# A third set of weight buffers, and weights fetched two ahead, in a two-layer attention and FFN trunk

## The chip, the cores and the metric

The kernel runs on one core of a Trainium2 chip. The metric is the device time of one execution in microseconds (us), as the median of several runs; a profile of one more execution shows where the time goes.

## What is computed

Two layers over a sequence of 512 tokens with a model width of 1024, all in float32. Each layer is a mixer and a gated FFN with a short causal convolution, each behind an RMS norm and added to x. The mixer of layer 0 is a sparse attention with three branches (compressed blocks, selected blocks, a window; NSA below), that of layer 1 a sliding-window attention (SWA). A last norm ends it. Cut from the reference:

```
for i in range(DEPTH):                       # DEPTH = 2
    h = rms_norm(x, norm_mix[i])
    x = x + (nsa_mixer(h, ...) if i % 2 == 0 else swa_mixer(h, ...))
    h = rms_norm(x, norm_ffn[i])
    x = x + conv_ffn(h, ffn_w_gu[i], ffn_conv_w[i], ffn_conv_b[i], ffn_w_down[i])
return rms_norm(x, norm_final)

def conv_ffn(h, w_gu, conv_w, conv_b, w_down):     # D_FF = 2816
    a, u = split(h @ w_gu, 2)
    a = causal_depthwise_conv(a, conv_w, conv_b)   # width 3
    return (silu(a) * u) @ w_down
```

## The kernel before, in words

x is held transposed, as eight chunks X[k] of 128 features x 512 tokens. A product in float32 is made of three matmuls in a reduced type (fp32r): every operand is split in a high part, its cast, and a low part, what the cast lost; then high x high, high x low part of x, and low part of the weight x high (`mm3_steps`, L200 to L207; its matmuls are L206). Chunks of x are split by L310 or L309 (`xh`) and L313 (`xl`).

**Weights.** `load_w` (L175 to L185) brings one weight of 128 x 1024: SP issues the transfer into a raw tile (`wraw`, L182, with a raised priority), ACT casts it to the high part (`wh`, L183), and DVE or POOL subtracts to the low part (`wl`, L184); `lo_eng`, or an argument, says which. The three tiles come from the pool `wp` (L148) with two buffers of each. In attention, weights come from a list `to_load` through `next_w` (L194 to L199), which hands out one and fetches the next. Elsewhere `load_w` is called where a weight is used: the first two weights of the kernel (L484), the two first products of each FFN (`first_products`), the plain gate/up products of each FFN (`plain`, L554, f = 0 to 3) and the down projection (`load_down`).

**The FFN's other products** (f = 4 on) follow a Strassen-like scheme with seven half-width products instead of eight: `operands` (L577 to L597) makes sums of chunks of the normed x on POOL (L585 to L588) and splits them (ACT L591, a copy into PSUM by ACT at L595, DVE L597 into `xs`); `weights(f)` (L599 to L621) makes sums of weights on POOL (L608), two of them into a tile with the tag `wraw`, casts them on ACT (L614) into a tile of the tag `wh` and others, and makes low parts on DVE (L620), of a copy in PSUM for some. So these sums use the pool `wp` too. TensorE multiplies at L631. After each gate/up product POOL multiplies the gate by the up part (L567 and its like at the end of `gate_up_7`).

**Order.** The code gives a program order and a few priorities; a scheduler then sets the order on every engine and queue, from dependencies, priorities and when the buffers of a tag come free. A buffer set that is larger changes where a load, its cast and its split stand among the other work. All transfers are issued by SP or ACT. Softmax heads in attention run with steps of weight products put in between (class `Fill`).

## Time and profile before

| | us |
|---|---|
| runs, median of 3 (lowest to highest) | 1260.33 (1257.42 to 1264.54) |
| profiled execution, its own time | 1261.37 |
| span of its profile | 1259.5 |
| busy in the span: TensorE (PE) | 1209.9 |
| busy: VectorE (DVE) | 890.4 |
| busy: ScalarE (ACT) | 788.3 |
| busy: GpSimd (POOL) | 565.1 |

The mean granted clock of TensorE is 0.993 of full speed. In the span the stages lie one after the other: the first loads and the norm to about 24 us, NSA to 348, a norm and the first FFN products to 375, the FFN to 730 (plain products to 410, seven-product scheme to 600, down projection after it), SWA from 735 to 866, and the second FFN to the end. SyncE (SP) only issues transfers. "Waits" below are idle times of an engine put down to what ended them; busy times count no waits.

### The profile page before, as it was taken

The page shows a single profiled execution, that of the slowest core. Times are in us where ns is not written, and L with a number is a line of the kernel's source. Part 1 is how long each engine was busy: PE and PEld are TensorE (multiplying, and loading weights), DVE is VectorE, ACT ScalarE, POOL GpSimd, SP SyncE. Part 2 cuts the span into 40 slices and gives each one's busy share as a digit, 9 for nine tenths or more (in the row PEclk, how much of TensorE's full clock was granted, in tenths as well). Part 3 has the DMA queues.
Part 4 walks back from the last instruction along what each step waited for, and adds up shares of the span by engine and source line. Part 5 has one row for each costly group of instructions (what it writes and reads, how often), then busy time and mean ns, then how long its engine had stood idle before and what let it go on. Part 6 is the DMA issues. An engine that isn't in the chain of part 4 may idle for free.

```text
span 1259.5 us, 20317 instructions
## 1 busy us (share of the span) xinstructions
PE 1209.9 (96%) x7174; PEld 1045.0 (83%) x7174; DVE 890.4 (71%) x1785; ACT 788.3 (63%) x1644; POOL 565.1 (45%) x441
## 2 busy tenths in 40 slices
PE   6999999999999899999999999999989999999997
PEld 4877996787878899999788887788779999988886
DVE  6476778878677988788633367997798887893223
ACT  4377676767559878878422225865688878873222
POOL 4295554534229566763000126322586667710002
PEclk9999999989999999999999999999999999999998
DMA  5856635041124323331233365422413333213333
GB/s 191 245 162 195 196 119 157 26 147 39 48 75 135 108 96 108 108 103 55 80 94 96 89 199 152 126 72 88 151 60 113 102 106 107 88 46 109 92 92 126
DMA packets 65910, 141.71 MB, mean 113 GB/s; under 512 B 8464, under 2 KB 16912, under 8 KB 65808
## 3 DMA queue, kind: packets, MB, share of 16 engines
q1 hardware_dynamic: 64432, 139.25, 35.9%
q8 instruction: 57, 0.93, 0.3%
q10 hardware_dynamic: 1376, 1.15, 0.3%
q14 instruction: 45, 0.37, 0.1%
HBM read 123.14 MB, written 17.24 MB: 111 GB/s over the span
## 4 chain that ended last, share of the span: by engine, by line
PE 67%; DVE 14%; issue 5%; DMA 5%; POOL 5%; ACT 4%; SPq 0%; POOLq 0%; ACTq 0%; DVEq 0%
PE mm L206 31%; PE mm L631 9%; PE s L631 7%; PE o L631 6%; DVE ls L620 2%; PE s L1177 1%; PE s L206 1%; PE t L1201 1%; PE o L1019 1%; DVE xl L313 1%; PE o L1322 1%; POOL wl L184 1%; DMA wraw<-in_w_gu 1%; DVE p L1196 1%; DVE p L1416 1%
## 5 line engine op out<-in xcount | busy, mean ns | idle before, releaser
L183 ACT CAST wh<-wraw 128x1024 fp32r<-128x1024 f32 (+3 forms) x136 | 126.2, 930 | 236.1 <-PE mm L206 143.3
L184 DVE TENSOR_TENSOR wl<-wraw,wh 128x1024 fp32r<-128x1024 f32 (+3 forms) x80 | 96.6, 1209 | 115.5 <-PE mm L206 68.6
L184 POOL TENSOR_TENSOR wl<-wraw,wh 128x1024 fp32r<-128x1024 f32 (+3 forms) x56 | 108.3, 1936 | 138.2 <-PE mm L206 77.0
L206 PE MATMUL mm<-xs,wh 128*128 128x512 f32 (+1 forms) x374 | 141.3, 383 | 2.3 <-DVE apad L635 2.3
L239 POOL TENSOR_TENSOR rt<-rt 128x512 f32<-128x512 f32 x22 | 31.5, 1430 | 197.7 <-ACT rt L233 197.5
L206 PE MATMUL mm<-xh,wh 128*128 128x512 f32 x264 | 107.3, 408 | 6.2 <-ACT wh L183 5.2
L206 PE MATMUL mm<-xl,wh 128*128 128x512 f32 x264 | 105.6, 401 | 3.8 <-DVE xl L313 3.8
L620 DVE TENSOR_TENSOR ls<-s,hs 128x512 fp32r<-128x512 f32 x72 | 90.4, 1266 | 3.1 <-ACT hs L614 1.9
L206 PE MATMUL mm<-xs,wl 128*128 128x512 f32 (+1 forms) x374 | 90.5, 382 | 0.0
L1187 ACT ACTIVATE p<-p,sm 128x128 f32<-128x128 f32 (+3 forms) x128 | 71.7, 562 | 22.7 <-DVE sm L1184 22.2
L631 PE MATMUL mm<-xs,hs 128*128 128x256 f32 x576 | 84.7, 284 | 0.5 <-DVE apad L635 0.5
L206 PEld LDWEIGHTS mm<-xs,wh 128*128 128x128 f32 x374 | 70.4, 188 | 17.4 <-DVE apad L635 2.7
L631 PE MATMUL o<-xs,ha 128*128 128x256 f32 x576 | 81.1, 283 | 1.9 <-ACT apad L641 1.9
L608 POOL TENSOR_TENSOR s<-u,u 128x512 f32<-128x512 f32 x36 | 48.5, 1347 | 72.8 <-DVE la L620 34.0
L206 PEld LDWEIGHTS mm<-xs,wl 128*128 128x128 f32 x374 | 67.6, 188 | 15.1
L631 PEld LDWEIGHTS mm<-xs,hs 128*128 128x128 f32 x576 | 76.0, 193 | 0.7 <-DVE apad L635 0.7
L631 PEld LDWEIGHTS o<-xs,ha 128*128 128x128 f32 x576 | 74.3, 192 | 2.5 <-ACT apad L641 2.3
L206 PE MATMUL mm<-xh,wl 128*128 128x512 f32 x264 | 70.1, 394 | 0.0
L1184 DVE CUSTOM_DVE_ANT_0 p<-s,cst 128x128 f32<-128x128 f32 (+3 forms) x128 | 58.5, 481 | 15.9 <-PE s L1177 8.6
L206 PEld LDWEIGHTS mm<-xh,wh 128*128 128x128 f32 x264 | 50.8, 193 | 17.4 <-ACT wh L183 5.2
L206 PEld LDWEIGHTS mm<-xl,wh 128*128 128x128 f32 x264 | 50.5, 192 | 15.6 <-DVE xl L313 6.3
L608 POOL TENSOR_TENSOR wraw<-a,u 128x512 f32<-128x512 f32 x36 | 57.3, 1591 | 7.4 <-ACT t L618 7.4
(369 smaller groups left out, 3538.4 us busy)
## 6 DMA issues: line engine op xcount, KB each, us to landing
u<-in_w_gu SPq DMA_DIRECT2D x72, 256.0 KB, 2.6
a<-in_w_gu SPq DMA_DIRECT2D x72, 256.0 KB, 2.7
wraw<-in_w_dn SPq DMA_DIRECT2D x34, 512.0 KB, 3.5
wraw<-in_w_nsa SPq DMA_DIRECT2D x19, 512.0 KB, 4.4
q<-d SPq DMA_DIRECT2D x32, 256.0 KB, 4.8
wraw<-in_w_gu SPq DMA_DIRECT2D x16, 512.0 KB, 3.7
wraw<-in_w_dn SPq DMA_DIRECT2D x17, 384.0 KB, 3.1
d<-rh SPq DMA_DIRECT2D x21, 256.0 KB, 2.4
```

Source lines behind the costliest of these rows:

```text
L183: nc.scalar.copy(wh[:, c], raw[:, c])
L184: (eng or lo_eng[0]).tensor_tensor(wl[:, c], raw[:, c], f32(wh[:, c]), op=ALU.subtract)
L206: nc.tensor.matmul(pt, ws[k][w], rs[k][r], start=first and i == 0, stop=last and i == len(ops) - 1, **kw)
L239: self.eng.tensor_tensor(self.acc, self.acc, sq, op=ALU.add)
L313: nc.vector.scalar_tensor_tensor(xl[k], xt, V(gain, k), f32(xh[k]), op0=ALU.mult, op1=ALU.subtract)
L608: nc.gpsimd.tensor_tensor(out, x, y, op=op)
L620: nc.vector.tensor_tensor(ws[o][1], w, f32(ws[o][0]), op=ALU.subtract)
L631: nc.tensor.matmul(pt, ws[o][w][:, i * P:(i + 1) * P], xs[:, o, i, x], start=start and n == 0, stop=n == len(ops) - 1, skip_group_check=True)
L1019: nc.tensor.matmul(acc[0][:, j * P:], v2[:, 2 * j + br], pp[:, 4 * j:4 * j + NT - j, :], start=br == 0 and j == 0 and pp is pts[0][0], sto ...
L1177: ins = nc.tensor.matmul(dst, ql, kk[:, :, :n] if shared else kk[:, br, :n], start=c.start == 0 and kk is kst[0], stop=kk is kst[-1], skip ...
L1184: nc.vector.tensor_tensor_reduce(pt[:, c], pss[:, c], mask[:, T - (c.stop - c.start):], -1.0, 3e38, ALU.add, ALU.min, st[:, u:u + 1])
L1187: nc.scalar.activation(pt[:, c], pt[:, c], AF.Exp, scale=-1.0, bias=st[:, u:u + 1], accum_out=st[:, 2 + u:3 + u])
```

## The change

The pool `wp` gets three buffers of each of its tags, 12 KB more per partition (3 tags x 128 x 1024 values of 4 bytes = 4 KB each), and the scratch that is kept for dynamic transfers is set to 4096. `next_w` fetches until two weights are loaded and not yet handed out, instead of one. As the same tags serve the FFN, its products have three sets as well. In the changed file, lines from L182 on stand one further down, and from L199 on two.

```diff
+W_BUFS = 3
...
-    wp = ctx.enter_context(tc.tile_pool(name="wp", bufs=2))
+    wp = ctx.enter_context(tc.tile_pool(name="wp", bufs=W_BUFS))
...
         w = loaded.popleft()
-        fetch_w()
+        while to_load and len(loaded) < W_BUFS - 1:
+            fetch_w()
         return w
...
-    nc = bacc.Bacc("TRN2", target_bir_lowering=False, num_devices=1)
+    nc = bacc.Bacc("TRN2", target_bir_lowering=False, num_devices=1, dynamic_dma_scratch_size=4096)
```

**Start of the kernel, SP's queue.** X are the eight chunks of x (L482, now L484), `wraw<-in_w_nsa` the raw weights (L182, now L183). Before:

```order
L482 DMA X<-in_x 128x512
L182 DMA wraw<-in_w_nsa 128x512 x2
L482 DMA X<-in_x 128x512
L182 DMA wraw<-in_w_nsa 128x1024
L482 DMA X<-in_x 128x512 x6
L182 DMA wraw<-in_w_nsa 128x1024
L487 DMA cst<-in_consts 128x384
```

Now:

```order
L484 DMA X<-in_x 128x512
L183 DMA wraw<-in_w_nsa 128x512 x2
L484 DMA X<-in_x 128x512
L183 DMA wraw<-in_w_nsa 128x1024
L484 DMA X<-in_x 128x512 x3
L183 DMA wraw<-in_w_nsa 128x1024
L484 DMA X<-in_x 128x512 x2
L183 DMA wraw<-in_w_nsa 128x1024
L484 DMA X<-in_x 128x512
L489 DMA cst<-in_consts 128x384
```

The third weight's load moved from behind all eight chunks to behind the fifth, and a fourth weight's load stands ahead of the eighth.

**Start of the kernel, DVE.** `xl_81` to `xl_88` are the low parts of chunks 0 to 7 (L313, now L315), `rt` the running sum of squares for the norm (L239, now L241), `wl` the low part of the third weight (L184, now L185). Before:

```order
L313 SCALAR_TENSOR_TENSOR xl_85<-X,vec,xh_77 128x512
L309 TENSOR_SCALAR xh_80<-X,vec 128x512
L313 SCALAR_TENSOR_TENSOR xl_88<-X,vec,xh_80 128x512
L239 TENSOR_TENSOR rt<-rt 128x512
L313 SCALAR_TENSOR_TENSOR xl_87<-X,vec,xh_79 128x512
L239 TENSOR_TENSOR rt<-rt 128x512 x3
L892 TENSOR_TENSOR ohl<-rt,ohl 128x8x48
L184 TENSOR_TENSOR wl<-wraw,wh 128x1024
```

Now:

```order
L315 SCALAR_TENSOR_TENSOR xl_86<-X,vec,xh_78 128x512
L185 TENSOR_TENSOR wl<-wraw,wh 128x1024
L241 TENSOR_TENSOR rt<-rt 128x512
L315 SCALAR_TENSOR_TENSOR xl_87<-X,vec,xh_79 128x512
L311 TENSOR_SCALAR xh_80<-X,vec 128x512
L241 TENSOR_TENSOR rt<-rt 128x512
L315 SCALAR_TENSOR_TENSOR xl_88<-X,vec,xh_80 128x512
L241 TENSOR_TENSOR rt<-rt 128x512
```

The third weight's split moved from behind the sums to ahead of the last two low parts of x, and one more sum stands ahead of the last. ACT's cast of that weight now stands ahead of the high part of the seventh chunk in the same way.

**Start of the first FFN, POOL.** `lu_4232<-ls_4230,ls_4231` (L588, now L590) is the last sum of the operands, `g` a gate product, L608 (now L610) sums of weights. Before:

```order
L608 TENSOR_TENSOR s_4332<-a_4328,wraw 128x512
L588 TENSOR_TENSOR lu_4232<-ls_4230,ls_4231 128x256
L608 TENSOR_TENSOR wraw<-s_4485,a_4481 128x512
L608 TENSOR_TENSOR wraw<-a_4481,u_4483 128x512
L567 TENSOR_TENSOR g_4226<-g_4226,y 128x512
L608 TENSOR_TENSOR s_4486<-a_4482,wraw 128x512
L608 TENSOR_TENSOR wraw<-a_4635,u_4637 128x512
```

Now:

```order
L610 TENSOR_TENSOR wraw<-s_4485,a_4481 128x512
L610 TENSOR_TENSOR wraw<-a_4481,u_4483 128x512
L589 TENSOR_TENSOR ls_4231<-ls_4230,ls_4231 128x256
L610 TENSOR_TENSOR s_4486<-a_4482,wraw 128x512
L569 TENSOR_TENSOR g_4226<-g_4226,y 128x512
L590 TENSOR_TENSOR lu_4232<-ls_4230,ls_4231 128x256
L610 TENSOR_TENSOR wraw<-a_4635,u_4637 128x512
```

Four operations that stood behind the last operand sum now stand ahead of it. Further up, the first weight split of this stage moved from behind to ahead of the first operand sum. On DVE the two low parts `ls_4365` and `ls_4369` (L620) stand ahead of the last `xs` (L597) in both orders.

**Start of the first FFN, TensorE.** `xs` are the operands, `s` and `mm` PSUM tiles; the row `s<-xs,wh` that stands alone last is the product with the last low part of an operand. Before:

```order
L631 MATMUL mm<-xs,wh 128x256 x7
L631 MATMUL s<-xs,wh 128x256 x7
L631 MATMUL mm<-xs,hs_4368 128x256
L631 MATMUL s<-xs,wh 128x256
L631 MATMUL mm<-xs,hs_4368 128x256 x7
```

Now:

```order
L633 MATMUL s<-xs,wh 128x256 x6
L633 MATMUL mm<-xs,hs_4368 128x256 x2
L633 MATMUL s<-xs,wh 128x256
L633 MATMUL mm<-xs,hs_4368 128x256 x6
L633 MATMUL mm<-xs,ls_4369 128x256 x4
L633 MATMUL s<-xs,wh 128x256
```

Ahead of that last product stood one matmul that did not need it; now there are twelve.

## Rows read from the trace of the kernel before

**Rows 1.** The page, busy time of each engine: us (share of the span) and instructions.

```profile
PE 1209.9 (96%) x7174; PEld 1045.0 (83%) x7174; DVE 890.4 (71%) x1785; ACT 788.3 (63%) x1644; POOL 565.1 (45%) x441
```

**Rows 2.** Windows: stretch, its us, busy PE, PEld, DVE, ACT, POOL, PEclk, DMA share, GB/s.

```profile
4.00:16.00 12.00, 7.17 (x17) 4.13 (x18) 9.37 (x8) 8.38 (x14) 8.23 (x5) 1.00 1.03 372
60.00:340.00 280.00, 271.36 (x1447) 221.45 (x1446) 216.45 (x626) 198.53 (x515) 141.83 (x123) 0.99 0.41 123
250.00:258.00 8.00, 6.30 (x22) 4.82 (x22) 6.68 (x20) 4.91 (x14) 7.34 (x7) 0.60 0.01 2
600.00:730.00 130.00, 130.00 (x566) 104.48 (x565) 52.84 (x58) 38.54 (x50) 13.64 (x9) 1.00 0.32 98
770.00:880.00 110.00, 107.05 (x597) 83.93 (x596) 97.00 (x304) 75.00 (x227) 37.69 (x31) 1.00 0.36 106
```

**Rows 3.** Waits of TensorE: who waited for whom, total us, times, longest us.

```profile
PE s L631 <- DVE xs L597: 5.2, 2, 2.7
...
PE s L1177 <- DVE sm L1184: 1.9, 2, 1.2
...
PE mm L631 <- DVE wl L620: 0.8, 1, 0.8
```

**Rows 4.** Waits of SP's DMA queue, in the same columns.

```profile
SPq L182 <- DVE wl L184: 330.7, 68, 15.9
SPq L182 <- POOL wl L184: 169.0, 37, 21.2
```

**Rows 5.** Timeline of DVE, 15 to 24 us: start us, us, operation [idle before <-releaser].

```profile
18.29 0.69 DVE L239 TENSOR_TENSOR rt<-rt 128x512 f32<-128x512 f32 x1
...
18.89 0.75 DVE L313 SCALAR_TENSOR_TENSOR xl<-X,vec,xh 128x512 fp32r<-128x512 f32 x1
...
22.57 1.22 DVE L184 TENSOR_TENSOR wl<-wraw,wh 128x1024 fp32r<-128x1024 f32 x1 [0.27 <-issue]
```

**Rows 6.** Timeline of TensorE, the same stretch.

```profile
19.69 0.50 PE L206 MATMUL mm<-xl,wh 128*128 128x512 f32 x1 [0.54 <-DVE xl L313]
```

**Rows 7.** Chain that ended last, NSA stage, 150 to 180 us: start us, us, what.

```profile
159.43 5.15 DMA wraw<-in_w_c
...
164.66 1.06 ACT wh L183
...
165.79 2.40 POOL wl L184
...
168.20 3.73 DMA wraw<-in_w_c
```

**Rows 8.** Timeline of TensorE, start of the first FFN, 410 to 417 us.

```profile
411.23 1.00 PE L631 MATMUL s<-xs,wh 128*128 128x256 f32 x7
...
415.05 0.39 PE L631 MATMUL s<-xs,wh 128*128 128x256 f32 x1 [2.71 <-DVE xs L597]
```

**Rows 9.** Timeline of DVE, the same place, 405 to 416 us.

```profile
408.29 6.11 DVE L620 TENSOR_TENSOR ls<-s,hs 128x512 fp32r<-128x512 f32 x2 [0.64 <-POOL lu L588]
...
414.32 0.68 DVE L597 TENSOR_TENSOR xs<-t,xs 128x512 fp32r<-128x512 f32 x1
```

**Rows 10.** Groups by line: busy us, mean ns of one, idle us before and its releasers.

```profile
L620 DVE TENSOR_TENSOR ls<-s,hs 128x512 fp32r<-128x512 f32 x72 | 90.4, 1266 | 3.1 <-ACT hs L614 1.9 <-POOL lu L588 1.3
...
L620 DVE TENSOR_TENSOR la<-t,ha 128x512 fp32r<-128x512 f32 x72 | 48.2, 686 | 7.6 <-ACT ha L614 6.0 <-ACT t L618 1.1
...
L608 POOL TENSOR_TENSOR wraw<-a,u 128x512 f32<-128x512 f32 x36 | 57.3, 1591 | 7.4 <-ACT t L618 7.4
```

**Rows 11.** Timeline of POOL, 370 to 416 us.

```profile
378.26 0.74 POOL L585 TENSOR_TENSOR hs<-ha 128x256 f32<-128x256 f32 x1 [4.24 <-DVE ha L581]
...
379.10 2.42 POOL L184 TENSOR_TENSOR wl<-wraw,wh 128x1024 fp32r<-128x1024 f32 x1
...
407.52 0.73 POOL L588 TENSOR_TENSOR lu<-ls,ls 128x256 f32<-128x256 f32 x1
...
411.99 1.26 POOL L608 TENSOR_TENSOR s<-a,wraw 128x512 f32<-128x512 f32 x1
```

## The prediction

> **What bounds the kernel now.** I read the busy table first, to see which engine fills the span; then the same in windows of one stage each, to see where that engine is not full; then what it waited for; then what the queue that fetches weights waited for, since that is what the change touches.

> TensorE (PE) is busy 1209.9 of 1259.5 us [rows 1]. The windows [rows 2] show the missing 50 us in pieces: down projections 130.00 of 130 us, so nothing can be won there; NSA attention 271.36 of 280; SWA attention 107.05 of 110. What is left lies at the start, at the norms between stages and at the end, which hang on sums and reciprocal roots, not on weights.

> SP's queue stands 330.7 + 169.0 = 499.7 us at the raw weight load L182, waiting until an older raw buffer has been split [rows 4]. That looks like what a third buffer set cures. But it is idle time of an engine that has nothing else to hurry for: among PE's waits [rows 3] the only one for a weight after the first microseconds that is worth a line is 0.8 us, once, for the low part made at L620. Weights come in time today. So the change can pay only through what loads, casts and splits do to the other work on ScalarE (ACT), VectorE (DVE) and GpSimd (POOL): the casts and splits now stand earlier in their queues.

> **The change, part by part.** No matmul, cast or split is added or removed. The sum is made against the profiled execution, 1261.37 us.

> *Scratch.* No transfer of this kernel is issued by POOL; all are on the SP and ACT queues. Nothing runs in the scratch that gives up room: 0.

> *Start.* In the new order the third weight's load goes ahead of X5, X6, X7, the fourth ahead of X7. The DMA engines are full there, 372 GB/s in 4 to 16 us [rows 2], so 0.52 MB more ahead delays X5 and X6 by 0.52 / 0.372 = 1.4 us and X7 by about twice that. The last low parts of x were made from 18.89 on [rows 5], and the eight X and four weights are 16 + 16 quarters of 0.13 MB, 4.2 MB in all, where the window alone moved 0.372 x 12 = 4.5 MB: they have landed by 16 us: hidden. What is not hidden is DVE. Before, the third weight's split took 1.22 us at 22.57, after the last low part of x, which ran at 18.89 with PE waiting for it until 19.69 [rows 5, 6]. Now the split and one more sum (0.60 us, the step from 18.29 to 18.89) stand ahead of the last two low parts. The last low part comes 1.22 + 0.60 = 1.8 us later, and PE has nothing else to do. From here to the next loose end PE is nearly full, so it stays lost. Bounds: 0, if DVE finds room in an earlier gap, to +1.9 + 1.06 (the ACT cast that now precedes the high part of X6 [rows 7]) = +3.0. I take **+1.8**.

> *The weight wait at L620.* Gone with a third set: **-0.8** (bounds -0.8 and 0).

> *Attention, NSA and SWA.* Here a fetch can hold up others: the chain of waits runs from 159.43 on through a weight's load (5.15), its cast (1.06), its POOL split (2.40) and the next load into the freed buffer (3.73) [rows 7]. With three sets the second load need not wait for the first split; its cast and split find their data landed and do not hold the softmax operations queued behind them. All that this can give is PE's idle time, 280 - 271.36 = 8.64 and 110 - 107.05 = 2.95 us, 11.6 in all [rows 2]. But none of PE's waits there is long; softmax's largest entry is 1.9 us in two [rows 3]; and DVE is 97.00 of 110 busy in SWA [rows 2]: softmax there waits for DVE itself, and a split done earlier is as long. Bounds: -11.6, and +3 for the same operations in a worse order (a quarter of that idle time). I take **-1.5**, about an eighth, nearer the small end because the waits for weights there are so few.

> *The clock.* [...] I take 0, bounds -2.5 and +2.5.

> *Both FFN starts.* PE waits 2.71 us, until 415.05, for the last operand split of L597, and 5.2 - 2.7 = 2.5 at the second layer [rows 3, 8]. That split starts at 414.32 behind two weight splits that took 6.11 us together [rows 9]; these have two operands in SBUF and take 1.266 us on average, the same operation on a copy in PSUM 0.686 [rows 10]. They overlap POOL's unbroken run from 407.52 to 411.99 + 1.26 = 413.25 [rows 11]. In the new order POOL does the four operations that followed the last operand sum, 413.25 - 408.25 = 5.0 us, *before* it, while one weight split (2.42) moves into the 4.24 us in which POOL sat idle ahead of 378.26 [rows 11]. So the sum ends between 408.25 + 5.0 - 2.4 = 410.9 and 413.3; two ACT passes (0.6 each, half of a double-width cast's 1.06 and a little) and the split of 0.68 follow: ready at 412.8 to 415.2, against 415.0. PE reached its wait at 415.05 - 2.71 = 412.3 and now has eleven more matmuls ahead of it (seven take 1.00 us [rows 8], eleven about 1.5): the wait begins at 413.8. If DVE is free, this start gains 1.3 to 2.7. If the two weight splits are held up by POOL as before, for 6.11 - 2 x 0.69 = 4.7 us, and POOL's run is longer by the wraw sum that no longer waits for a buffer (7.4 us of such waits in all, 1.591 a piece [rows 10]), the operand comes up to 4.7 later than 415.2, 419.9, and the start loses 419.9 - 413.8 - 2.7 = 3.4. I take **-1.0** for the pair, on the gaining side because the eleven matmuls are certain and the hold-up is not; bounds -5.2 and +6.8.

> [...]

> *Norms between the stages.* DVE is the engine there; a split of 1.22 [rows 5] that moves across one changes it by that at most, either way: 0.

> *Down projections, Strassen products, end.* Earlier fetches, same PE work, no PE wait for them: 0. The cover is PE's full run; if it went, one load costs 3.73 [rows 7].

> **Sum:** 1261.37 + 1.8 - 0.8 - 1.5 - 1.0 = 1259.9. The median of the three runs, 1260.33, lies 1.04 below the profiled execution; less that, **1258.8 us**. A measurement of this kernel can tell about 0.5%, 6.3 us, from no change.

> **Rivals.**
> *It pays (1251).* The fetch two ahead takes the waits at the head of ACT's and DVE's queues out of attention. For it: SP's 499.7 us [rows 4] and a chain that goes through two loads in a row [rows 7]. Against it: PE's few waits for weights [rows 3]. With 5 of the 11.6 us idle, the 2.5 of the clock, one FFN start's 2.7 and the 0.8 won, and 1.8 lost at the start: 1260.3 - 9.2 = 1251.1.

> *It costs (1268).* POOL at the two FFN starts, as worked out above: its operations stand without a gap ahead of the last operand sum and hold up DVE's two-operand splits, which stand ahead of the last operand split. It decides where that split ends after 413.8 + 2.7 = 416.5 on the clock of the run before. With 2.7 lost at each start (most of the bound of 3.4), the 1.8 of the first microseconds, and nothing won elsewhere: 1260.3 + 7.2 = 1267.5. For it: [rows 9 to 11]. Against it: the eleven matmuls of cover, and POOL's idle time, now filled.

> *It does not do what it says (1260).* The raw loads are issued earlier, but splits and casts still run in the scheduler's old places. The order at the start speaks against it. It would be no change.

> **How the numbers follow.** Forecast 0.52; not done 0.04; it pays 0.24; it costs 0.20. PE's 1209.9 us of unchanged work and its few waits for weights hold the forecast; the bounds of attention (-11.6) and of the FFN starts (-5.2 and +6.8) reach beyond 6.3 us on both sides. Faster means under 1254.0: most of "it pays" (0.18) and the low tail of the forecast (0.05), 0.23. Slower means above 1266.6: most of "it costs" (0.15) and the forecast's high tail (0.05), 0.20. No change 0.57. The range of 8 in 10 leaves a tenth out on each side: 1249.5 to 1268.

> **What the profile of the changed kernel would show.** Right: PE's wait for the last low part of x ends near 21.5 instead of 19.69; SP's wait at the raw load is shorter, by a third or so of 499.7, with the span hardly moved; PE busy stays near 1210; the attention windows gain 1 to 2 us of PE's idle time; PE's wait at the FFN starts for L597 is under 2.7. Wrong: under 5 us idle left in the attention stages (it pays); waits for L597 above 4 us with the two weight splits over 6 us ahead of them (it costs); a granted clock below 0.99 in a stage that had 1.00; or a new PE wait for a cast at L183, which would mean that a fetch now stands ahead of what it should follow.

## The result and the profile after

The changed kernel is slower: 1273.45 us as the median of six runs (1270.92 to 1276.55), against 1260.71 for six runs of the kernel before on the same chip. The ratio is 1.0109, 95% interval 1.0088 to 1.0129. The prediction, 1258.8 with a range up to 1268.0, was wrong in its sign and missed the range by 5.5 us. The profiled execution took 1270.92 us; its span is 1269.1 us, against 1259.5, and its mean granted clock 0.987, against 0.993.

The busy table of the changed kernel stands against [rows 1]:

```profile
PE 1217.7 (96%) x7174; PEld 1051.0 (83%) x7174; DVE 884.4 (70%) x1785; ACT 787.0 (62%) x1644; POOL 561.8 (44%) x441
```

The same 7174 matmuls kept TensorE (PE) busy 7.8 us longer. Idle time grew from 49.6 to 51.4. So of 9.6 us more span four fifths are matmuls that took longer, and it is worth asking where they did, before asking what PE waited for.

Windows of the changed kernel: the place in NSA that answers to 250 to 258 us in [rows 2], the first down projection's start, the part of SWA in [rows 2], then the whole stretch from the first norm's matmuls to the first FFN, and the whole of SWA. Columns are the stretch, its us, busy PE, PEld, DVE, ACT, POOL, then PEclk, DMA share, GB/s:

```profile
258.00:266.00 8.00, 7.77 (x30) 6.09 (x29) 6.18 (x22) 4.26 (x13) 5.56 (x7) 0.64 0.01 2
600.00:609.00 9.00, 6.37 (x16) 5.04 (x17) 9.00 (x16) 4.01 (x8) 0.00 (x0) 0.62 0.16 46
770.00:880.00 110.00, 104.88 (x578) 82.12 (x577) 98.47 (x308) 76.69 (x235) 38.89 (x33) 0.98 0.36 104
...
25.00:366.40 341.40, 330.70 (x1722) 270.14 (x1721) 249.24 (x667) 220.20 (x544) 156.65 (x132) 0.99 0.44 129
730.05:894.37 164.32, 159.12 (x829) 126.22 (x828) 128.51 (x349) 96.21 (x260) 57.22 (x42) 0.99 0.42 123
```

The kernel before, in the two stretches that answer to the last two:

```profile
22.30:360.40 338.10, 329.38 (x1722) 269.00 (x1721) 246.21 (x667) 218.71 (x544) 159.60 (x132) 0.99 0.44 131
...
724.38:883.84 159.46, 156.51 (x830) 124.95 (x828) 128.57 (x349) 95.47 (x260) 57.71 (x42) 1.00 0.42 129
```

The slow place of [rows 2] at 250 us has only moved, with all that stands ahead of it, to 258 us (clock 0.64). New is that in 600 to 609 us, where the kernel before had TensorE full, it is busy 6.37 of 9 us at a granted clock of 0.62. The stretch to the first FFN has the same 1722 matmuls in 3.3 us more, 2.0 of them idle and 1.3 busy. SWA, from its first product to the second FFN's, takes 4.9 us more for the same products, 2.3 idle and 2.6 busy.

Waits of TensorE in the changed kernel (who waited for whom, total us, times, longest us), against [rows 3]:

```profile
PE mm L208 <- DVE apad L637: 6.6, 2, 3.3
...
PE s L1396 <- DMA kl<-d: 1.8, 1, 1.8
PE s L1179 <- DMA kh<-d: 1.7, 1, 1.7
...
PE s L633 <- DVE xs L599: 0.2, 1, 0.2
```

The wait for the operand split, 5.2 us before, and the weight wait of 0.8 are as good as gone. What stands first now is a pair of waits of 3.3 us for a sum of DVE, L637. [rows 3] did not list it, but in the kernel before it was there too, a third as long:

```profile
PE mm L206 <- DVE apad L635: 2.3, 2, 1.2
```

Those two lie at the end of the gate/up products, one in each FFN. TensorE in the changed kernel, the first of them (start us, us, operation, in brackets the idle time ahead):

```profile
598.69 0.64 PE L633 MATMUL mm<-xs,ls 128*128 128x256 f32 x4
602.63 0.80 PE L208 MATMUL mm<-xs,wh 128*128 128x512 f32 x1 [3.30 <-DVE apad L637]
603.23 0.63 PE L208 MATMUL mm<-u,wh 128*128 128x512 f32 x1
603.65 0.63 PE L208 MATMUL mm<-xs,wh 128*128 128x512 f32 x1
...
609.14 2.03 PE L208 MATMUL mm<-xs,wl 128*128 128x512 f32 x8
```

The same place in the kernel before:

```profile
599.15 0.50 PE L206 MATMUL mm<-xs,wh 128*128 128x512 f32 x1 [1.13 <-DVE apad L635]
599.49 0.40 PE L206 MATMUL mm<-u,wh 128*128 128x512 f32 x1
599.72 0.39 PE L206 MATMUL mm<-xs,wh 128*128 128x512 f32 x1
...
602.99 2.02 PE L206 MATMUL mm<-xs,wl 128*128 128x512 f32 x8
```

The hole is 3.30 instead of 1.13 us, and what follows it is slow: steps of 0.43 us (603.23 to 603.65), at a granted clock of 0.50 in 603 to 606 us, where they were 0.23 us (599.49 to 599.72), at 1.00 in 599.15 to 602.99 us. Sixteen products take 609.14 - 602.63 = 6.51 us, before 602.99 - 599.15 = 3.84. In the second FFN the hole is 3.33 for 1.17 us, and the sixteen products take 5.32 for 3.85.

What DVE did ahead of and in that hole, in the changed kernel:

```profile
596.40 2.23 DVE L685 TENSOR_TENSOR u<-g,xs 128x512 fp32r<-128x512 f32 x2
598.56 1.28 DVE L685 TENSOR_TENSOR a<-xh,xs 128x512 fp32r<-128x512 f32 x2
599.76 1.28 DVE L685 TENSOR_TENSOR ha<-xh,xs 128x512 fp32r<-128x512 f32 x2
600.97 1.28 DVE L685 TENSOR_TENSOR la<-xl,xs 128x512 fp32r<-128x512 f32 x2
602.17 0.41 DVE L637 TENSOR_TENSOR apad<-mm,apad 128x256 f32<-128x256 f32 x1
```

L637 adds the last product to its half of the output and frees the PSUM tile that the down projection needs. Between the last weight split (L622 at 595.80) and this sum stand eight low parts of gated chunks (L685), without a gap; the last product was done by 599.4. In the kernel before there are three low parts and a step of the convolution in that place, and the two `la` run behind the sum, at 599.00:

```profile
596.21 0.69 DVE L683 TENSOR_TENSOR u<-g,xs 128x512 fp32r<-128x512 f32 x1
596.81 0.76 DVE L549 SCALAR_TENSOR_TENSOR s<-apad,conv_t,s 128x512 f32<-128x512 f32 x1
597.47 1.30 DVE L683 TENSOR_TENSOR ha<-xh,xs 128x512 fp32r<-128x512 f32 x2
598.67 0.43 DVE L635 TENSOR_TENSOR apad<-mm,apad 128x256 f32<-128x256 f32 x1
599.00 1.29 DVE L683 TENSOR_TENSOR la<-xl,xs 128x512 fp32r<-128x512 f32 x2
```

Landmarks turn all this into an account. Parts of the profiled executions in us: "start" to the first norm's matmul, NSA to the first product of the FFN, each FFN to the first eight low-part products of its down projection, and between them the rest of the down projection and SWA. "Scratch" is the kernel before with the scratch edit alone (below), whose order is that of before.

| | before | scratch | after | after less before |
|---|---|---|---|---|
| start | 22.31 | 22.49 | 24.96 | +2.65 |
| NSA | 338.06 | 336.88 | 341.40 | +3.34 |
| first FFN | 242.62 | 239.82 | 242.78 | +0.16 |
| down, SWA | 280.85 | 281.46 | 285.23 | +4.38 |
| second FFN | 242.01 | 242.91 | 241.86 | -0.15 |
| rest | 133.65 | 133.34 | 132.87 | -0.78 |
| span | 1259.5 | 1256.9 | 1269.1 | +9.6 |

The FFNs look untouched and are not: up to the hole, without it, they became 4.68 and 3.78 us shorter, and hole and slow products gave back 4.84 and 3.63. In the stretch between them SWA makes all of the loss; the down projection is 0.5 us shorter.

### The profile page after: what moved, and what is told of

Same layout as the page of the kernel before. It is cut to its first block, busy times and chain, and to the rows that moved or that the text cites. A ratio compares the mean times of both kernels' runs of the same rounds, so it can differ in the third digit from the quotient of the medians.

```text
span 1269.1 us, 20303 instructions
## 1 busy us (share of the span) xinstructions
PE 1217.7 (96%) x7174; PEld 1051.0 (83%) x7174; DVE 884.4 (70%) x1785; ACT 787.0 (62%) x1644; POOL 561.8 (44%) x441
## 4 chain that ended last, share of the span: by engine, by line
PE 70%; DVE 12%; POOL 5%; DMA 5%; issue 3%; ACT 3%; SPq 1%; POOLq 0%; DVEq 0%; ACTq 0%
PE mm L208 31%; PE mm L633 10%; PE s L633 7%; PE o L633 7%; PE s L1179 2%; PE t L1203 2%; PE o L1021 2%; DMA d<-rh 1%; DVE p L1418 1%; DVE xl L315 1%; DVE ls L622 1%; PE s L208 1%; POOL wl L185 1%; PE o L1324 1%; POOL s L610 1%
## 5 line engine op out<-in xcount | busy, mean ns | idle before, releaser
L184 ACT CAST wh<-wraw 128x1024 fp32r<-128x1024 f32 (+3 forms) x136 | 126.5, 930 | 240.3 <-PE mm L208 157.1
L185 POOL TENSOR_TENSOR wl<-wraw,wh 128x1024 fp32r<-128x1024 f32 (+3 forms) x56 | 107.5, 1921 | 169.8 <-ACT wh L184 64.5
L185 DVE TENSOR_TENSOR wl<-wraw,wh 128x1024 fp32r<-128x1024 f32 (+3 forms) x80 | 94.2, 1177 | 108.2 <-PE mm L208 72.3
L208 PE MATMUL mm<-xs,wh 128*128 128x512 f32 (+1 forms) x374 | 143.9, 390 | 6.6 <-DVE apad L637 6.6
L241 POOL TENSOR_TENSOR rt<-rt 128x512 f32<-128x512 f32 x22 | 30.0, 1365 | 215.1 <-ACT rt L235 200.8
L622 DVE TENSOR_TENSOR ls<-s,hs 128x512 fp32r<-128x512 f32 x72 | 81.1, 1140 | 7.5 <-ACT hs L616 4.5
L610 POOL TENSOR_TENSOR s<-u,u 128x512 f32<-128x512 f32 x36 | 50.0, 1389 | 37.9 <-DMA u<-in_w_gu 30.4
L208 PEld LDWEIGHTS mm<-xl,wh 128*128 128x128 f32 x264 | 51.4, 195 | 16.4 <-DVE xl L315 6.8
L610 POOL TENSOR_TENSOR wraw<-a,u 128x512 f32<-128x512 f32 x36 | 57.2, 1589 | 9.9 <-DMA a<-in_w_gu 9.9
```

Of the source, the lines that this page charges most:

```text
L184: nc.scalar.copy(wh[:, c], raw[:, c])
L185: (eng or lo_eng[0]).tensor_tensor(wl[:, c], raw[:, c], f32(wh[:, c]), op=ALU.subtract)
L208: nc.tensor.matmul(pt, ws[k][w], rs[k][r], start=first and i == 0, stop=last and i == len(ops) - 1, **kw)
L241: self.eng.tensor_tensor(self.acc, self.acc, sq, op=ALU.add)
L610: nc.gpsimd.tensor_tensor(out, x, y, op=op)
L622: nc.vector.tensor_tensor(ws[o][1], w, f32(ws[o][0]), op=ALU.subtract)
```

## The experiments

Ratios are to the kernel before on the same chip, with 95% intervals. My theory after the result: a third set in the FFNs makes the scheduler put DVE work that waits for a buffer under two sets ahead of what TensorE needs. (The low parts of gated chunks are not in tiles of `wp`, so the third set acts on them through other work; how, no run here shows.) The rivals: the deeper fetch is at fault; the scratch costs; or the order of the kernel before was tuned for two sets and any other order is worse.

**Scratch alone**, two sets:

```diff
+    nc = bacc.Bacc(..., dynamic_dma_scratch_size=4096)
```

> The kernel before with the smaller scratch alone; every engine's order is the same as before. Theory A and all others but one: 1258 us, the same as before. Rival G (the smaller scratch slows something): 1265 us or more.

1259.31 us, ratio 1.0010 (0.9994 to 1.0027). The scratch costs nothing. Its waits carry a second lesson:

```profile
PE s L631 <- DVE xs L597: 2.2, 1, 2.2
```

The order of all engines is that of before, yet one of the two waits for the operand split of [rows 3] is missing: in the first FFN the two weight splits ahead of that operand took 3.48 us here, against 6.11 in [rows 9].

```profile
407.26 3.48 DVE L620 TENSOR_TENSOR ls<-s,hs 128x512 fp32r<-128x512 f32 x2 [0.63 <-POOL lu L588]
```

That wait is an event of the run as much as of the order, and 2.8 us of what the changed kernel's first FFN won are within it.

**Fetch one ahead**, three sets:

```diff
-        while to_load and len(loaded) < W_BUFS - 1:
-            fetch_w()
+        fetch_w()
```

> Three buffer sets and the small scratch as in the change, but next_w fetches one weight ahead as before. Theory A (the third buffer set itself lets the scheduler put loads, casts and splits of weights ahead of work that TensorE waits for; the fetch depth hardly matters): as slow as the change, 1272 to 1275 us. Rival B (the second weight fetched ahead does the damage): back near 1261 us.

1275.12 us, ratio 1.0126 (1.0098 to 1.0155): no better. The orders of TensorE, ACT and POOL are those of the change. The `while` of the change is not what costs; the buffers are.

**The third set held back.** An unused tile of each tag, written once, keeps one set out of use through a stage (six small operations of GpSimd), so that the stage has two as before:

```diff
+    def pin():
+        for n, t in (("wraw", F32), ("wh", F32R), ("wl", F32R)):
+            pinned.append(wp.tile([P, 1024], t, name=n, tag=n))
+            nc.gpsimd.memset(... pinned[-1][:, 0:1] ..., 0.0)
+    def unpin(x):
+        for t in pinned:
+            nc.gpsimd.tensor_tensor(pin_to, t[:, 0:1], x[:, 0:1], op=ALU.add)
```

Through the FFNs:

> The change, but one buffer set is held by an unused tile from the start of each FFN to its seventh down projection, so FFNs run on two sets and attention on three. Theory A from the two traces: attention stages lost 6.0 us up to the first FFN and 5.0 from there to the second, FFNs won about 1 us net: 1271 to 1274 us, with TensorE's wait for the sum into apad at the end of the FFN products back at about 1.2 and its wait for the last operand split back at 2.7. Rival C (the FFN's own third set is what costs): near 1262 us.

Through the attention stages:

> The change, but one buffer set is held by an unused tile from the start of each attention stage to its last residual, so attention runs on two sets and FFNs on three. Theory A: the 11 us of the attention stages come back, 1259 to 1263 us. Rival C: still near 1272 us. Rival D (any new order of the scheduler costs some us, whichever stage has the set): both this and the one with two sets in the FFNs come out about half way, 1266 us.

Through both:

> The change with the third set held by an unused tile in every stage (nine small operations on POOL a stage): two sets to work with everywhere, but the scheduler's order differs from before in a few hundred rows. Theory A (the third set puts splits ahead of what TensorE waits for): 1258 to 1262 us. Rival D (any other order of the scheduler costs, with two sets as well): 1266 to 1272 us.

FFNs 1.0113 (1.0082 to 1.0143), attention 1.0093 (1.0067 to 1.0119), both 1.0029 (1.0010 to 1.0048). With every stage back on two sets nearly three quarters of the loss are gone, though the scheduler's order is then not that of before either. Its profile says where: the FFNs take 244.52 + 236.08 us, 4.0 less than in the change, and NSA is back at 337.49, but down and SWA take 286.30, 1.1 more than in the change. So SWA's loss stays with two sets as well. One by one neither does it, and the landmarks say in part why: with two sets in the FFNs the two FFNs take 239.18 + 239.79 us, 5.7 less than in the change, but down and SWA take 287.03; with two sets in attention NSA is back at 336.41, but the FFNs take 489.1 and SWA stays at 286.31. The first profile is also the quickest of its six runs, 1267.76 against a median of 1272.50, so its FFNs may show more gain than its median has. Attention on two sets, forecast at 1259 to 1263 us, took 1270.68.

The wait at the end of the products is back at its old length when the FFNs have two sets, in the run with the FFNs alone and in the run with both, whose row this is:

```profile
PE mm L221 <- DVE apad L655: 2.3, 2, 1.2
```

**The sum first.** Splits of gated chunks from 8 on, high and low parts, are issued behind the sum that frees the PSUM tile:

```diff
-            add(ar, pd, ar)
+            freed[0] = add(ar, pd, ar).ins
...
-                    split_g(c0 + j)
+                    with tc.issue_after(freed[0]) if c0 else nullcontext():
+                        split_g(c0 + j)
```

> The change, but at the end of each FFN's gate/up products the splits of gated chunks 8 and up may only be issued after the sum into apad that frees the PSUM bank of the first down projection. Theory E (TensorE's 3.3 us wait there, and the half clock behind it, come from DVE doing these splits ahead of that sum): the wait falls to about 1 us in both layers, the stretch at half clock behind it goes, 6 to 8 us won: 1265.5 to 1268 us. Rival F (the product before it is what is late; the order of DVE there is not the cause): no change, 1273 us.

1266.97 us, ratio 1.0069 (1.0044 to 1.0093): 0.4% of the 1.1% back by an edit of order alone. TensorE at the place:

```profile
606.22 0.50 PE L208 MATMUL mm<-xs,wh 128*128 128x512 f32 x1 [1.56 <-DVE apad L639]
606.55 0.40 PE L208 MATMUL mm<-u,wh 128*128 128x512 f32 x1
606.79 0.40 PE L208 MATMUL mm<-xs,wh 128*128 128x512 f32 x1
```

The hole is half as long, and after it the products run in steps of 0.24 us: no slow stretch.

**The hole filled.** Twelve matmuls whose result nobody uses stand between the last gate/up product and the down projection:

```diff
+                for _ in range(N_IDLE):
+                    with tc.issue_after(last_product[0]):
+                        ins = nc.tensor.matmul(idle, gh[0][:, :P], gh[0], start=True, stop=True)
```

> The change with twelve idle matmuls (128x512, 2.8 us at full clock; their result is not used) on TensorE in the hole between the last gate/up product and the first down projection of each FFN. Theory K (of the 4.9 and 3.2 us lost there, the part behind the hole is the clock that fell while TensorE idled): the hole itself stays, the stretch at half clock behind it goes, 2 x 1.2 to 2 x 2.5 us won, 1266.5 to 1269 us. Rival (the clock falls for another reason, or the matmuls only stand in the way): 1271.5 us or more.

1270.54 us, ratio 1.0105 (1.0082 to 1.0129), no gain that the intervals can tell, and over the forecast of 1266.5 to 1269. The trace shows that the slow stretch is the hole's doing, not the work's:

```profile
602.50 2.91 PE L715 MATMUL t<-xs 128*128 128x512 f32 x12
606.16 0.51 PE L209 MATMUL mm<-xs,wh 128*128 128x512 f32 x1 [0.76 <-DVE apad L642]
606.50 0.40 PE L209 MATMUL mm<-u,wh 128*128 128x512 f32 x1
606.74 0.40 PE L209 MATMUL mm<-xs,wh 128*128 128x512 f32 x1
```

DVE is as late as before, but the products after it take steps of 0.24 us, not 0.43. The second FFN is 1.4 us shorter than in the change, what its slow stretch had cost. In the first FFN the gain is lost again ahead of the hole: up to the last product it takes 236.5 us, in the change 233.0. No run here shows why.

**Three raw sets only**, two of the high and low parts:

```diff
+        wh = wp.tile([P, 1024], F32R, name="wh", tag="wh", bufs=2)
+        wl = wp.tile([P, 1024], F32R, name="wl", tag="wl", bufs=2)
```

> The change, but three buffers for raw weights only, two for high and low parts: transfers early, casts and splits no earlier than before. Theory A, in the words of splits: the start, NSA's rope and the keys of SWA come back, 8 to 11 us won against the change, 1260 to 1264 us. Rival H (early transfers of weights hold up the round trips of keys and queries through DRAM): still 1270 us or more, with a wait of TensorE for kh, kl or X from a transfer of over 1 us.

> raw_three, with the splits of gated chunks 8 and up behind the sum into apad as in adds_first. Theories A and E together: 1254 to 1260 us; at or under the kernel before if the 2.5 us at both FFN starts stay won. Rival D: 1266 us or more.

1.0096 (1.0076 to 1.0116), and with the sum first too 1.0070 (1.0045 to 1.0094). Weights that are only loaded earlier, not split earlier, are no cure. The start, however, is:

```profile
19.19 0.75 DVE L315 SCALAR_TENSOR_TENSOR xl<-X,vec,xh 128x512 fp32r<-128x512 f32 x1
...
22.50 1.22 DVE L185 TENSOR_TENSOR wl<-wraw,wh 128x1024 fp32r<-128x1024 f32 x1
```

The third weight's split stands behind the last low part of x again, and the norm's matmuls begin at 22.16 instead of 24.96 us. So the cast and the split make the loss there, not the load; with the split alone held back (next) they begin at 22.92, against 24.38 with one weight fetched ahead and no hold.

The holes at the end of the products lie between those of two and of three sets here, first and second FFN:

```profile
600.10 0.50 PE L208 MATMUL mm<-xs,wh 128*128 128x512 f32 x1 [2.34 <-DVE apad L637]
1127.78 0.70 PE L208 MATMUL mm<-xs,wh 128*128 128x512 f32 x1 [2.37 <-DVE apad L637]
```

After the first, the sixteen products take 3.84 us, as in the kernel before; after the second, 5.38.

**Splits held back.** One ahead; a weight's split is not issued ahead of the last low part of x at the start, of the end of a query's rope in NSA, of the keys' rope in SWA (where the change has put 1.21 us of weight split into it):

```diff
+            with tc.issue_after(hold[0]) if hold[0] is not None else nullcontext():
+                (eng or lo_eng[0]).tensor_tensor(wl[:, c], raw[:, c], f32(wh[:, c]), op=ALU.subtract)
```

> The change with one weight fetched ahead, and the low-part split of a weight may not be issued ahead of the last low part of x at the start, of the end of the last rotation begun before its fetch (on the same engine), or of the end of the rotation of SWA's keys. Theory A, place by place: 2.5 us at the start, some 3 in NSA and 3 to 4 at the keys of SWA come back against the change, 1262 to 1266 us where the kernel before runs in 1257.5 and the change, by its ratio, in 1271.5. Rival D: 1270 us or more, the holes only move.

> late_splits and adds_first together. If theories A and E hold and their places add up: 1256 to 1261 us, no slower than before by more than 0.3%. Rival D: 1266 us or more.

1.0174 (1.0150 to 1.0199), the worst of all; with the sum first as well 1.0081 (1.0055 to 1.0107). A row of the first's waits:

```profile
PE s L958 <- DMA q<-d: 5.1, 1, 5.1
```

A new wait for a transfer of queries, 5.1 us at 278 us, came with the held splits. The wait for the keys' low parts in SWA stayed at 2.0 us, so the split in the rope was not its cause; I had read that from the order alone. That wait for `kl` is 1.8 to 2.4 us in all ten kernels with three sets of high and low parts in attention, and 0.8 or less in the nine others. It is a mark of the third set, but not what makes SWA long: attention on two sets is without it and takes as long there. With the sum first, both FFNs take 238.36 + 239.15 us, 7.1 less than in the change.

Five forecasts that rested on my theory for attention missed, by 6 to 14 us: attention on two sets, three raw sets without and with the sum first, splits held back without and with it. Three of the five times lie where the rival "any other order costs" had put them.

**Other orders, with two and with three sets.** To learn whether the loss is one of three sets or of the constants that were chosen with two, three other sets of constants, each on both kernels: how fast attention's filling work is handed out (fill), which low parts GpSimd makes (lo), and of the latter the FFN's alone (plo5).

```diff
-RATE_NSA = (4.2, 2.8, 1.5, 2.2)
+RATE_NSA = (4.0, 2.9, 1.6, 2.2)
-WARM_NSA, WARM_SWA = (54, 66)
-RATE_SWA = (2.7, 2.1, 4.1, 4.4)
+WARM_NSA, WARM_SWA = (48, 72)
+RATE_SWA = (2.6, 2.2, 4.1, 4.4)
...
-LO_NSA = (1, 3, 6, 12, 15, 16, 18, 20, 23, 33)
-LO_SWA = (1, 5, 7, 15, 16, 19, 26)
+LO_NSA = (1, 3, 6, 12, 15, 16, 18, 21, 23, 33)
+LO_SWA = (1, 5, 8, 15, 16, 19, 26)
-PLO = ((3, 6, 7), (3, 6, 7))
+PLO = ((3, 5, 7), (3, 5, 7))
```

> The kernel before, two sets, with other constants for how many projection steps are put among the softmax heads (WARM 48 and 72, RATE 4.0, 2.9, 1.6, 2.2 and 2.6, 2.2, 4.1, 4.4): the same work in another order. Theory A (the third set is bad in itself): within 0.4% of before, 1257 to 1263 us. Rival D (any other order costs): 1266 to 1274 us.

> The change with the constants of two_fill. Theory A: about 12 us above two_fill, 1270 to 1276 us. Rival D: about as two_fill, within 5 us either way.

> The kernel before, two sets, with three of its splits given to the other of DVE and POOL (LO_NSA 21 for 20, LO_SWA 8 for 7, PLO 5 for 6). Theory A: 1257 to 1263 us. Rival D: 1264 to 1272 us.

> The change with the splits given out as in two_lo. Theory A: about 12 us above two_lo, 1269 to 1276 us. Rival D: about as two_lo, within 5 us either way.

> The kernel before, two sets, with one low part of a plain FFN weight made by GpSimd for another (product 5 in place of 6, both layers). Attention's order is as before; at both FFN starts three products, not one, stand between the start of the last operand's stretch and the product that waits for it. If the order of the FFN alone sets the wait for the last operand split (5.2 us in two), it shrinks to under 3, attention keeps its 338 and 281 us, and the time is 1253 to 1257, ratio 0.994 to 0.998: faster than both. If the wait is what DVE and GpSimd make of each other and not of the place, the wait stays near 5 and the ratio is 0.999 to 1.001.

> The change, three sets, with the same other product. If the third set's price in the FFNs is the hole at the end of the gate/up products, that hole is there again (over 6 us in two waits) and the two FFNs take 484 to 491 us to the low-part products of the first down weights, 5 to 11 more than two sets with the same constant; ratio 1.008 to 1.014. If the price was a chance of the one constant, the FFNs are within 3 us of those of two sets and the ratio is under 1.006.

| constants | two sets | three sets | both FFNs, two | three | wait for the sum, two | three |
|---|---|---|---|---|---|---|
| as before | 1 | 1.0109 | 484.6 | 484.6 | 2.3 | 6.6 |
| fill | 1.0041 (1.0022 to 1.0061) | 1.0141 (1.0120 to 1.0162) | 477.1 | 488.1 | 2.3 | 7.5 |
| lo | 1.0075 (1.0050 to 1.0100) | 1.0142 (1.0110 to 1.0174) | 476.4 | 490.5 | 2.3 | 7.3 |
| plo5 | 1.0015 (0.9994 to 1.0036) | 1.0144 (1.0111 to 1.0176) | 482.5 | 490.0 | 2.3 | 6.7 |

Three sets are 0.7 to 1.3% slower in every pair, by the quotient of the two ratios, and the wait for the sum goes from 2.3 to about 7 us in every one. On two sets its row stands in the trace of fill as it stands in that of the kernel before; on three it is:

```profile
PE mm L208 <- DVE apad L637: 7.5, 2, 4.2
```

So the hole belongs to three sets and not to one table of constants. The FFNs lose 11.0, 14.1 and 7.5 us in the three new pairs, of which longer holes and slow products behind them make 8.2, 9.1 and 8.6. In the first pair the kernel before had its own waits of 5.2 us at the FFN starts, and the loss hides behind their going. That gain does not belong to three sets: with lo and plo5 the kernels with three wait 3.4 and 3.0 us for the operand split, those with two not at all and 2.5. The start loses 1.0 to 2.8 us in all four. Attention does not follow the sets: NSA is 3.3 and 1.7 us longer with three in two pairs, 1.0 and 4.6 shorter in the others; down and SWA are 4.4, 0.4 and 4.7 us longer in three pairs, 1.3 shorter with lo. On two sets, too, NSA is 7 to 8 us longer with fill and lo than with the constants of before, and SWA with lo is longer than in the change. So the rival of the tuned order holds in part: other orders on two sets cost 0.15 to 0.75%, and three sets cost more on top of it. No version beat the kernel before: plo5 on two sets, meant to, kept one wait of 2.5 us for the operand split and is no faster.

## Why the prediction was wrong

**Start.** Right in kind. It took +1.8 for the low part of x that comes later; PE's wait for it ended at 21.21, forecast "near 21.5", 1.5 us later than before. The rows of the changed kernel, DVE and then TensorE, against [rows 5, 6]:

```profile
17.02 1.22 DVE L185 TENSOR_TENSOR wl<-wraw,wh 128x1024 fp32r<-128x1024 f32 x1
...
20.41 0.74 DVE L315 SCALAR_TENSOR_TENSOR xl<-X,vec,xh 128x512 fp32r<-128x512 f32 x1
```

```profile
19.55 0.50 PE L208 MATMUL mm<-xl,wh 128*128 128x512 f32 x1 [1.43 <-DVE xl L315]
...
21.21 0.61 PE L208 MATMUL mm<-xl,wh 128*128 128x512 f32 x1 [0.77 <-DVE xl L315]
21.62 3.50 PE L208 MATMUL mm<-xh,wl 128*128 128x512 f32 x8
24.96 0.28 PE L251 MATMUL t<-ones,rt 128*128 128x1 f32 x2
```

The term measured +2.65: eight low-part products behind the waits took 3.50 us, at a granted clock of 0.52 in 21.5 to 25 us, where the kernel before has 1.99, at 1.00 in 20 to 22 us. The clock was missing from the term.

**The weight wait, -0.8, and the FFN starts, -1.0.** Both waits went, as forecast (0.2 us is left). The eleven matmuls of cover did half of it in the first FFN. Counted from the stage's first product, TensorE came to the waiting product 1.3 us later than before, and the operand was ready 1.3 us earlier, because the two weight splits ahead of it took 1.30 us and not 6.11 [rows 9]. They stand behind GpSimd's last sum now, and GpSimd then does nothing until 422.10:

```profile
417.22 1.30 DVE L622 TENSOR_TENSOR ls<-s,hs 128x512 fp32r<-128x512 f32 x2 [1.36 <-POOL lu L590]
```

```profile
419.77 0.39 PE L633 MATMUL s<-xs,wh 128*128 128x256 f32 x1 [0.15 <-DVE xs L599]
421.03 0.74 PE L633 MATMUL o<-xs,la 128*128 128x256 f32 x4 [0.87 <-DVE la L622]
```

So the hold-up by GpSimd that the rival "It costs" and its 1267.5 assumed did not come here; that rival had the wrong place. The last row is a wait that is new, for the low part of a weight: 1.5 us in both FFNs together. The FFNs up to their last product gained more than the term, 8.5 us, of which up to 2.8 lie within what two runs of one order differ by.

**"Down projections, Strassen products, end: 0".** This step failed. It read the cover as "PE's full run" and priced its loss as one load, 3.73 us. But TensorE's start of the down projection hangs on a PSUM tile that DVE frees (it waited 3.30 and 3.33 us for L637), and DVE's order there was not looked at. Its term is +8.5 us at the two ends: 2.17 + 2.16 more hole and 2.67 + 1.47 of slow products. It took back the gain of the FFNs ahead of it, to within 0.1 us; that the two are so nearly equal is chance, as the other pairs show.

**Attention, -1.5, bounds -11.6 and +3.** Wrong in sign and outside its bounds: +3.3 in NSA and +4.4 in the stretch of the down projection and SWA, 7.7 together. The reason given, that softmax waits for DVE itself, spoke for no gain; it did not bound a loss. The loss is idle time (2.0 in NSA, 2.3 in SWA) and matmuls that took longer (1.3 and 2.6), but what makes it is not settled. Two waits for transfers of keys are new, 1.7 and 1.8 us, but holding the splits back left the second as long and brought a longer wait elsewhere; SWA is as long without that wait; and other orders on two sets lose as much in NSA.

**The clock, 0, bounds -2.5 and +2.5.** No run shows the 2.5 us of these bounds, which the rival "It pays" counted as won. The slow stretch of [rows 2], 250 to 258 us at a granted clock of 0.60, stayed: 0.64 in 258 to 266 us now. The step did not ask whether new ones would come. TensorE's busy time rose by 7.8 us in the profiled executions with no matmul added, and in the FFN ends one sees it happen: after a hole of 3.3 us matmuls run in steps of 0.43 us for 0.23, at a granted clock of 0.50 in 603 to 606 us, for 1.5 to 2.7 us of extra time; after the holes of 1.1 to 1.7 us at this place, or one filled with idle products, they do not. It happens in attention too, behind a wait for a transfer that was 0.64 us before and is 1.56 now; the granted clock is 0.72 in the 6 us that follow:

```profile
113.05 0.49 PE L833 MATMUL mm<-wh,X 128*124 128x256 f32 x1 [1.56 <-DMA X<-d]
```

In 770 to 880 us the clock is 0.98, where [rows 2] has 1.00: a sign that the prediction had named for being wrong. In 600 to 609 us, the stretch with the first of the holes in the FFNs, it is 0.62, where the kernel before has 1.00.

**SP's wait.** "Shorter by a third or so" was wrong too; the queue waits at the raw loads 332.0 + 205.6 = 537.6 us, against 499.7 in [rows 4]:

```profile
SPq L183 <- DVE wl L185: 332.0, 64, 15.3
SPq L183 <- POOL wl L185: 205.6, 37, 21.8
```

Here the third buffer only let the queue run one load further ahead and wait there. That it cost nothing either way had been said rightly.

**The sum.** The forecast's terms were 1.8 - 0.8 - 1.5 - 1.0 = -1.5. Measured, in the same parts: 2.65 at the start, 7.7 in attention, -8.5 and +8.5 in the FFNs, -0.8 after them: +9.6. The chance of 0.20 for a slower kernel went to a mechanism that is not what happened; the bound of attention's loss, a quarter of its idle time, was chosen from idle time alone, while 1.3 and 2.6 us of the measured loss are matmuls that took longer.

## What to carry to other kernels

Where weights come in time already, a further buffer brings forward the loads, casts and splits, and with them other work, on engines that the bottleneck waits for elsewhere: go through the order of each such engine at every place where the bottleneck changes its kind of work, and see what now stands ahead of the operation that releases it, PSUM tiles included. Price a new hole of TensorE with the matmuls behind it too, not with its length alone: here, behind holes of 3.30 to 4.18 us, they came in steps of 0.43 us for 0.23, which cost 1.3 to 2.7 us more. And compare both versions under a few other constants before you call a difference that of the edit: here the pairs showed what one pair hid.

## What the runs showed of the hardware

One order of instructions, run twice, waited for the same operand split 2.7 us in one execution and not at all in another. The two weight splits ahead of it took 6.11 us in the one and 3.48 in the other. So a single wait of that size is no property of a kernel.
